# Block sums of the second feed-forward weight: from VectorE subtractions to accumulating transfers issued by GpSimd

## The chip, the cores and the metric

The kernel runs on one core of one Trainium2 chip. The metric is the device time of one execution in microseconds (us). TensorE (PE) multiplies, VectorE (DVE) and ScalarE (ACT) work element by element, GpSimd (POOL) does little in this kernel, and SyncE (SP) issues the transfers from device memory into SBUF. Each engine works through its own queue in order and waits for others through semaphores.

## What is computed

Two layers on 256 tokens of 1024 values in float32. Each layer is a feed-forward block at half weight, a token mixer (a state-space branch and a gated delta-rule branch), and a second feed-forward block; a normalisation closes the whole. Only the feed-forward blocks are touched by the change:

```python
def swiglu(x, w_in, w_out):
    gate, up = jnp.split(x @ w_in, 2, axis=-1)
    return (jax.nn.silu(gate) * up) @ w_out
...
for l in range(DEPTH):
    h = h + 0.5 * swiglu(rms_norm(h, ffn1_norm[l]), ffn1_w_in[l], ffn1_w_out[l])
    ...
    h = h + 0.5 * swiglu(rms_norm(h, ffn2_norm[l]), ffn2_w_in[l], ffn2_w_out[l])
```

`w_in` is 1024 x 5632 and `w_out` 2816 x 1024, so there are four feed-forward blocks in one execution.

## The kernel before

**Weights and forms.** Weights come as tiles of 128 x 1024 float32 (512 KB). Each product is made from two halves of a weight in the matmul's rounded type: `whi` is the tile rounded by ACT (`act(hi[:], r[:])`, line 163) and `wlo` the rest, `r - hi`, by DVE (line 170). Such a pair is called a form here. PE uses a form in three matmuls per place (`mm3`, lines 295 to 298; `mm3w`, lines 300 to 303). The forms of the whole program are listed ahead in `plan`, the tiles that have to be loaded in `stream`.

**Queues.** `take()` (line 182) hands PE the next form. It first calls `load` for the tiles that the form five places on will need and four more, and then `prep` for the forms up to five places on (`NSPL = 5`). Raw tiles lie in a ring of five (`NRAW = 5`, tile `wraw`), the halves in rings of five `whi` and five `wlo`. So a load can start when the form of the tile five loads earlier has been prepared, and a form can be prepared when PE has finished the form five places before it. SP issues all loads. A compile-time scheduler may put an instruction earlier in its engine's queue than program order if its buffer is free.

**One feed-forward block.** The string `FFN` (line 37) gives the order of the work: `f`, four forms for the first columns of `w_in`; twenty `c` (`chan_chunk`), each 48 matmuls of 256 columns on two forms; and `w_out` in between and behind.

**The seven products.** `w_out` is cut into 22 blocks of 128 rows by two halves of 512 columns. Sixteen of the row blocks are done by Winograd's form of Strassen's scheme: for a pair of 2 x 2 block products there are four weight tiles w11, w12, w22, w21 and seven products instead of eight. `A` in `FFN` makes the first four (tiles `p`, forms q0 to q3), `B` the last three (forms q4 to q6, into the accumulators `o`). There are four `A` and four `B` in a block, 16 of each in the program. A product is one form and six matmuls of 512 columns (`block_products`). Row blocks that are left over are the six `d`, each one form and twelve matmuls. The forms that have to be made of weights are, in order, w11, w12 - w11, w22 - w12, w11 - w12 + w22, then w22, w21, and w21 - (w11 - w12 + w22). These sums of weights are made in place by DVE in `prep`: `less` (line 155) overwrites one raw tile with the difference of two, once each at q0, q1, q2 and q4. w11 lies in one of four extra tiles, `wfirst` (tags y0 to y3 of `slots`, shared with the mixer), and carries the running sum from q0 to q6. w22 is loaded twice, for `A` and for `B`.

**The sums of the input** are made by `block_sums` (line 449) on DVE and split into halves. `join` (line 388) adds the four banks `p` to the residual `h`, in two steps between the `B`s.

**The tail of a block.** After the last `c` come `B d B B B` and the five last `d`, `close_blocks` (line 404): 132 matmuls of 512 columns, before the next normalisation's transposes (`hnT`). Its rows carry the tile name `o`. In the normalisation POOL computes one power (line 190), on which the next block's input waits.

Of the kernel before, what the change touches and what calls it, by code (L numbers as in the profile page):

```python
# [7 lines left out]
F32 = mybir.dt.float32  # L8
# [3 lines left out]
ALU = mybir.AluOpType  # L12
# [4 lines left out]
P = 128  # L17
# [6 lines left out]
FC = FF // 256  # L24
# [5 lines left out]
NRAW = 5  # L30
NSPL = 5
# [5 lines left out]
FFN = "f" + 8 * "c" + "A" + 4 * "c" + "A" + 4 * "c" + "A" + 2 * "c" + "A" + 2 * "c" + "BdBBBddddd"  # L37
PAIRS = [(1, 2), (3, 4), (5, 6), (7, 8)]
# [14 lines left out]
def trunk_kernel(ctx, tc, x, wst, wsm, norms, lpar, rpar, cst, out):  # L53
    nc = tc.nc
    V, A, G, PE = nc.vector, nc.scalar, nc.gpsimd, nc.tensor
# [3 lines left out]
    slots = ctx.enter_context(tc.tile_pool(name="slots", bufs=1))  # L59
# [9 lines left out]
    def tt(o, a, b, op):  # L69
        return V.tensor_tensor(out=o, in0=a, in1=b, op=op)  # L70

    def stt(o, a, s, b, op0, op1):
        return V.scalar_tensor_tensor(out=o, in0=a, scalar=s, in1=b, op0=op0, op1=op1)  # L73
# [12 lines left out]
    def trb(name):  # L86
        return trp.tile([P, 512], F32, tag="tr", name=name)
# [10 lines left out]
    plan, stream = [], []  # L98

    def plan_plain(j, n):  # L100
        for i in range(j, j + n):
            stream.append(i)
            plan.append(("d", [len(stream) - 1], len(stream)))
        return j + n

    def plan_ffn(j):


        o, j2, held = j + 4 * FC, j + 4 * FC + 22, []
        for kind in FFN:  # L110
            if kind in "fc":
                j = plan_plain(j, 4 if kind == "f" else 2)
            elif kind == "d":
                o = plan_plain(o, 1)
            else:
                if kind == "A":
                    where = [len(stream) + i for i in range(3)]
                    stream.extend(range(o, o + 3))
                    held.append((where, o + 2))
                    o += 4  # L120
                    for i, need in enumerate((2, 3, 3, 3)):
                        plan.append((f"q{i}", where, where[0] + need))
                else:
                    where, b22 = held.pop(0)
                    where += [len(stream) + 1, len(stream)]
                    stream.extend([b22, b22 + 1])
                    for i in range(4, 7):
                        plan.append((f"q{i}", where, len(stream)))
        return j2

    j0 = 0
# [1 line left out]
        j0 = plan_ffn(plan_plain(plan_ffn(j0), mix))  # L133
    assert j0 == n_dram
    n_raw = len(stream)
    first = {js[0] for kind, js, _ in plan if kind == "q0"}
    n_forms = len(plan)
    state = {"loaded": 0, "prepped": 0, "taken": 0, "last": None, "hold": False, "behind": {}, "first": 0}
    raws, halves = {}, {}

    def load(j):
        if j in first:
            r = slots.tile([P, 1024], F32, tag=f"y{state['first']}", name="wfirst")
            state["first"] = (state["first"] + 1) % 4
        else:
            r = wpool.tile([P, 1024], F32, tag="wraw", name="wraw", bufs=NRAW)
        state["last"] = nc.sync.dma_start(r[:], wst[stream[j] // 2, :, (stream[j] % 2) * 1024 :][:, 0:1024])
        raws[j] = r

    def prep(i):  # L150
        kind, js, _ = plan[i]
        hi = wpool.tile([P, 1024], F32R, tag="whi", name="whi", bufs=NSPL)
        lo = wpool.tile([P, 1024], F32R, tag="wlo", name="wlo", bufs=NSPL)

        def less(o, a, b):
            tt(raws[js[o]][:], raws[js[a]][:], raws[js[b]][:], ALU.subtract)


        r = raws[js[{"q2": 1, "q4": 4, "q5": 3}.get(kind, 0)]]
        with ExitStack() as behind:  # L160
            for ins in state["behind"].pop(i, ()):
                behind.enter_context(tc.issue_after(ins))
            act(hi[:], r[:])
            if kind == "q1":
                less(1, 2, 1)
            elif kind == "q2":
                less(0, 2, 0)
            elif kind == "q4":
                less(0, 3, 0)
            tt(lo[:], r[:], f(hi[:]), ALU.subtract)  # L170
            if kind == "q0":
                less(0, 1, 0)
        for o in {"d": (0,), "q2": (1,), "q3": (2,), "q4": (4,), "q5": (3,), "q6": (0,)}.get(kind, ()):
            raws.pop(js[o])
        halves[i] = (hi, lo)

    def ahead(key, n, fn):
        while state[key] < n:
            fn(state[key])
            state[key] += 1  # L180

    def take():
        j = state["taken"]
        state["taken"] = j + 1
        ahead("loaded", min(plan[min(j + NSPL, n_forms) - 1][2] + NRAW - 1, n_raw), load)
        ahead("prepped", min(j + 1 if state["hold"] else j + NSPL, n_forms), prep)
        return halves.pop(j)

# [199 lines left out]
    def join(pb):  # L388

        hv = [[h[:, t, n * 512 : (n + 1) * 512] for n in range(2)] for t in range(2)]  # L390
        half, u2, u4, u5 = (tmp2(n) for n in ("half", "u2", "u4", "u5"))
        act(half[:], pb[1][:], scale=0.5)
        stt(hv[0][0], pb[1][:], 0.5, hv[0][0], ALU.mult, ALU.add)
        stt(u2[:], pb[6][:], 0.5, half[:], ALU.mult, ALU.add)
        stt(u4[:], pb[5][:], 0.5, u2[:], ALU.mult, ALU.add)
        tt(hv[0][1], hv[0][1], u4[:], ALU.add)
        yield
        stt(u2[:], pb[7][:], 0.5, u2[:], ALU.mult, ALU.add)
        stt(u5[:], pb[5][:], 0.5, u2[:], ALU.mult, ALU.add)
        tt(hv[1][0], hv[1][0], u2[:], ALU.add)  # L400
        tt(hv[1][1], hv[1][1], u5[:], ALU.add)
        yield

    def close_blocks(po, stat, sums, pb, nw):
# [24 lines left out]
    def ffn(nxt):  # L429
# [10 lines left out]
        def sums(p, j):  # L440

            q, i = (p - 1) // 2, (p - 1) % 2
            if j < 3:
                b = (bsa[:], bsb3)[q % 2]
                return b[:, i, 0, j, :], b[:, i, 1, j, :]
            b = (bsc[:, 0:2], bsc[:, 2:4], bsb1, bsd[:])[q]
            return b[:, i, 0, :], b[:, i, 1, :]

        def block_sums(p, g2):

            sf = tmp2("sf")
            a11, a21, a12, a22 = (g2[:, j * P : (j + 1) * P] for j in range(4))
            s1, s2_, s3, s4 = (sf[:, j * P : (j + 1) * P] for j in range(4))
            tt(s1, a21, a22, ALU.add)
            tt(s3, a11, a21, ALU.subtract)
            tt(s2_, s1, a11, ALU.subtract)
            tt(s4, a12, s2_, ALU.subtract)
            q, i = (p - 1) // 2, (p - 1) % 2
            h3, l3 = ((bsa[:], bsb3)[q % 2][:, i, o] for o in range(2))
            h1, l1 = sums(p, 3)  # L460
            s3v = sf[:, 0 : 3 * P].rearrange("p (j t) -> p j t", j=3)
            act(h3, s3v)
            act(h1, s4)
            tt(l3, s3v, f(h3), ALU.subtract)
            tt(l1, s4, f(h1), ALU.subtract)
# [7 lines left out]
        def stat(k, t):  # L473
            return (gh[k // 8][:, k % 8, t * P : (t + 1) * P], gl[k // 8][:, k % 8, t * P : (t + 1) * P])
# [10 lines left out]
        for c in range(FC - 1):  # L485
            g2 = tmp2("g2")
            for a in range(2):
                ps = accb("fc")
                chan_chunk(ps)
                sg = s2.tile([P, S], F32, tag="ca", name="sg", bufs=2)  # L490
                act(sg[:], ps[:, 0:S], AF.Silu)
                tt(g2[:, a * S : (a + 1) * S], sg[:], ps[:, S : 2 * S], ALU.mult)
                todo = todo[1:]
                if c == 0 and a == 0:
                    bank = trb("gT")
                    for k in range(2):
                        for t in range(2):
                            PE.transpose(bank[:, k * S + t * P : k * S + (t + 1) * P], gt[t][:, k * P : (k + 1) * P], ident)
                    split(0, bank[:].rearrange("p (k t) -> p k t", k=2))
            split(2 * c + 2, g2[:].rearrange("p (k t) -> p k t", k=2))  # L500
            if c + 1 <= PAIRS[-1][-1]:
                block_sums(c + 1, g2)
            if todo[0] == "A":
                if not pb:
                    pb.update({i: trb(f"p{i}") for i in (1, 6, 5, 7)})
                four = [
                    (pb[1], lambda p: stat(2 * p, 0), PAIRS[n]),
                    (pb[5], lambda p: sums(p, 0), PAIRS[n]),
                    (pb[7], lambda p: sums(p, 2), PAIRS[n]),
                    (pb[6], lambda p: sums(p, 1), PAIRS[n]),  # L510
                ]
                block_products(four, n == 0, n == len(PAIRS) - 1)
                todo = todo[1:]
                n += 1
# [844 lines left out]
```

## Time and profile before

| | us |
|---|---|
| median of three runs | 1576.33 (1573.42 to 1577.17) |
| the profiled execution, its own time | 1574.73 |
| its span in the profile | 1573.0 |
| PE busy in the span | 1544.0 |
| DVE busy | 1254.2 |
| ACT busy | 950.7 |
| POOL busy | 53.8 |

The span is what lies between the first and the last instruction; 1.7 us lie around it. A matmul's end in the profile is modelled and the next one begins before it, so PE's busy time hides short waits. The pace of PE is read from the starts of its matmuls.

### The profile page before, as it was taken

How to read it: one execution, taken by the hardware profiler on the slowest of the kernel's cores; microseconds unless marked ns; L12 is line 12 of the kernel's file. 1: busy time of each engine (PE TensorE's matmuls, PEld its weight loads, DVE VectorE, ACT ScalarE, POOL GpSimd, SP SyncE). 2: the span in 40 equal slices, each digit the busy share in tenths (PEclk: the TensorE clock that was granted, in tenths of full speed). 3: DMA queues.
4: the chain of work that ended last, by engine and by line, in shares of the span. 5: the costliest groups of instructions: out<-in, count | busy, mean ns of one | idle time of the engine just before them, and what ended most of it. 6: DMA issues, size and time to landing. Idle time of an engine off the chain costs nothing.

```text
span 1573.0 us, 28904 instructions
## 1 busy us (share of the span) xinstructions
PE 1544.0 (98%) x11432; PEld 1393.4 (89%) x11432; DVE 1254.2 (80%) x1888; ACT 950.7 (60%) x1534; POOL 53.8 (3%) x60
## 2 busy tenths in 40 slices
PE   8999999999999999999999999999999999999997
PEld 7999779999888888999789997899998888899995
DVE  6878868967899766878777888699589987677887
ACT  5656568766666645555555566776756665455554
POOL 0000010000000000000000001010000000000000
PEclk9999999999999999999999999999999999999999
DMA  8565565553565566565765456555345556555554
GB/s 297 199 201 186 185 213 188 168 164 114 180 212 164 183 205 192 169 207 181 243 206 191 166 186 223 192 188 188 115 137 200 175 185 215 176 191 187 161 186 133
DMA packets 94221, 293.12 MB, mean 186 GB/s; under 512 B 22325, under 2 KB 23301, under 8 KB 93062
## 3 DMA queue, kind: packets, MB, share of 16 engines
q1 hardware_dynamic: 94086, 291.29, 56.5%
q8 instruction: 89, 1.46, 0.4%
q14 instruction: 46, 0.38, 0.1%
HBM read 289.33 MB, written 1.92 MB: 185 GB/s over the span
## 4 chain that ended last, share of the span: by engine, by line
PE 68%; DVE 14%; DMA 7%; issue 5%; ACT 4%; POOL 1%; SPq 0%; POOLq 0%; ACTq 0%; DVEq 0%
PE fc L301 9%; PE fc L302 9%; PE fc L303 9%; DVE wlo L70 7%; DMA wraw<-in_wst_dram 4%; PE b L298 3%; PE t L297 3%; PE t L296 2%; PE t L298 2%; PE b L297 2%; PE b L296 2%; DVE ca L73 2%; ACT whi L67 2%; PE p L297 2%; PE p L298 2%
## 5 line engine op out<-in xcount | busy, mean ns | idle before, releaser
L70 DVE TENSOR_TENSOR wlo<-wraw,whi 128x1024 fp32r<-128x1024 f32 x488 | 592.3, 1222 | 176.8 <-ACT whi L67 172.3
L67 ACT ACTIVATE whi<-wraw 128x1024 fp32r<-128x1024 f32 x488 | 511.9, 1060 | 276.9 <-PE fc L302 96.0
L301 PE MATMUL fc<-uW,whi 128*128 128x256 f32 x1280 | 359.2, 281 | 0.0
L303 PE MATMUL fc<-uW,wlo 128*128 128x256 f32 x1280 | 358.9, 280 | 0.0
L302 PE MATMUL fc<-uW,whi 128*128 128x256 f32 x1280 | 358.9, 280 | 0.0
L303 PEld LDWEIGHTS fc<-uW,wlo 128*128 128x128 f32 x1280 | 243.6, 190 | 0.0
L301 PEld LDWEIGHTS fc<-uW,whi 128*128 128x128 f32 x1280 | 241.7, 189 | 0.8
L302 PEld LDWEIGHTS fc<-uW,whi 128*128 128x128 f32 x1280 | 240.3, 188 | 0.8
L67 ACT ACTIVATE whi<-wfirst 128x1024 fp32r<-128x1024 f32 x64 | 68.0, 1062 | 65.9 <-PE fc L302 50.9
L296 PE MATMUL t<-whi,uW 128*128 128x512 f32 x256 | 102.1, 400 | 0.0
L297 PE MATMUL t<-wlo,uW 128*128 128x512 f32 x256 | 100.6, 393 | 0.4 <-DVE wlo L70 0.4
L298 PE MATMUL t<-whi,uW 128*128 128x512 f32 x256 | 100.7, 393 | 0.0
L70 DVE TENSOR_TENSOR wlo<-wfirst,whi 128x1024 fp32r<-128x1024 f32 x64 | 78.3, 1223 | 8.8 <-ACT whi L67 8.8
L296 PE MATMUL b<-whi,bh 128*128 128x512 f32 x192 | 76.3, 399 | 0.3 <-ACT bh L67 0.2
L297 PE MATMUL b<-wlo,bh 128*128 128x512 f32 x192 | 74.9, 390 | 0.0
L298 PE MATMUL b<-whi,bl 128*128 128x512 f32 x192 | 74.3, 394 | 0.6 <-DVE bl L70 0.6
L70 DVE TENSOR_TENSOR wfirst<-wraw,wfirst 128x1024 f32<-128x1024 f32 x48 | 58.7, 1222 | 19.1 <-DMA wraw<-in_wst_dram 18.7
L301 PE MATMUL xs<-uW,whi 128*128 128x256 f32 x256 | 72.7, 284 | 0.0
L297 PE MATMUL o<-wlo,gh 128*128 128x512 f32 x160 | 64.5, 403 | 7.1 <-DVE wlo L70 6.9
L303 PE MATMUL xs<-uW,wlo 128*128 128x256 f32 x256 | 71.1, 278 | 0.0
L302 PE MATMUL xs<-uW,whi 128*128 128x256 f32 x256 | 71.0, 277 | 0.0
L296 PE MATMUL o<-whi,gh 128*128 128x512 f32 x160 | 62.1, 392 | 0.3 <-ACT whi L67 0.3
(315 smaller groups left out, 3385.8 us busy)
## 6 DMA issues: line engine op xcount, KB each, us to landing
wraw<-in_wst_dram SPq DMA_DIRECT2D x504, 512.0 KB, 4.5
wfirst<-in_wst_dram SPq DMA_DIRECT2D x16, 512.0 KB, 6.1
dc<-rdram SPq DMA_DIRECT2D x8, 1024.0 KB, 8.5
nw<-in_norms_dram SPq DMA_DIRECT2D x6, 512.0 KB, 5.9
gb<-rdram SPq DMA_DIRECT2D x8, 256.0 KB, 5.5
h<-in_x_dram SPq DMA_DIRECT2D x4, 256.0 KB, 5.9
out_dram<-fo SPq DMA_DIRECT2D x4, 256.0 KB, 2.0
dq<-X SPq DMA_DIRECT2D x2, 256.0 KB, 5.4
```

The lines of the kernel that those rows point to most:

```text
L67: return A.activation(out=o, in_=i, func=func, **kw)
L70: return V.tensor_tensor(out=o, in0=a, in1=b, op=op)
L73: return V.scalar_tensor_tensor(out=o, in0=a, scalar=s, in1=b, op0=op0, op1=op1)
L296: PE.matmul(ps, lh, rh, start=start, stop=False)
L297: PE.matmul(ps, lh, rl, start=False, stop=False)
L298: return PE.matmul(ps, ll, rh, start=False, stop=stop)
L301: PE.matmul(ps, wh, mh, start=start, stop=False)
L302: PE.matmul(ps, wh, ml, start=False, stop=False)
L303: PE.matmul(ps, wl, mh, start=False, stop=stop)
```

## The change

Every sum of weights now has plus signs only, so that it can be formed by transfers that add to what lies in the destination (`accum_op=ALU.add`), issued from POOL's queue. The signs move to the sums of the input (`block_sums`) and to `join`. The forms become: q1 = w11 + w12, q0 = w11, q2 = w12 + w22, q3 = w11 + w12 + w22, q4 = w22, q5 = w21, q6 = w11 + w12 + w22 + w21.

The running sum lies in the tile `wsum` (the four y tiles again): loaded with w11 two `c` ahead of its `A` in the stream, w12 added to it by a transfer at once, w22 after q1's halves are made, w21 after q3's. A ring tile `u` is loaded with w12, and w22 is added to it. w11 is loaded a second time, for q0. So a group of seven products has five plain loads, as before, and four adding transfers; and `less` is gone. `A` now takes its forms in the order q1, q0, q2, q3. In the stream an entry is "w" (ring load), "y" (load of a sum tile) or "+" (adding transfer); the load limit counts only "w" against the ring of five.

```diff
     def plan_ffn(j):
-        o, j2, held = j + 4 * FC, j + 4 * FC + 22, []
-        for kind in FFN:
+        o, j2, begun, held = j + 4 * FC, j + 4 * FC + 22, [], []
+        spots, q = [], 0
+        for at, kind in enumerate(FFN):
+            if kind == "A":
+                spots.append(at - 2)
+        o1 = o + FFN[: FFN.index("A")].count("d")
+        for at, kind in enumerate(FFN):
+            if at in spots:
+                y = len(stream)
+                stream.extend([("y", o1 + 4 * q), ("+", o1 + 4 * q + 1, y)])
+                begun.append(y)
+                q += 1
...
+            elif kind == "A":
+                y, u = begun.pop(0), len(stream)
+                stream.extend([("w", o + 1), ("+", o + 2, u), ("w", o)])
+                plan.append(("q1", (y, o + 2), u))
+                plan.append(("q0", (u + 2,), u + 3))
+                plan.append(("q2", (u,), u + 3))
+                plan.append(("q3", (y, o + 3), u + 3))
+                held.append((y, o + 2))
+                o += 4
             else:
-                if kind == "A":
-                    where = [len(stream) + i for i in range(3)]
-                    stream.extend(range(o, o + 3))
-                    held.append((where, o + 2))
-                    o += 4
-                    for i, need in enumerate((2, 3, 3, 3)):
-                        plan.append((f"q{i}", where, where[0] + need))
-                else:
-                    where, b22 = held.pop(0)
-                    where += [len(stream) + 1, len(stream)]
-                    stream.extend([b22, b22 + 1])
-                    for i in range(4, 7):
-                        plan.append((f"q{i}", where, len(stream)))
+                y, b22 = held.pop(0)
+                stream.append(("w", b22))
+                plan.append(("q4", (len(stream) - 1,), len(stream)))
+                stream.append(("w", b22 + 1))
+                plan.append(("q5", (len(stream) - 1,), len(stream)))
+                plan.append(("q6", (y,), len(stream)))
...
+    def add_to(r, i):
+        G.dma_start(out=r[:], in_=tile_of(i), accum_op=ALU.add)
+
     def load(j):
-        if j in first:
-            r = slots.tile([P, 1024], F32, tag=f"y{state['first']}", name="wfirst")
+        kind, i = stream[j][:2]
+        if kind == "+":
+            add_to(raws[stream[j][2]], i)
+            return
+        if kind == "y":
+            r = slots.tile([P, 1024], F32, tag=f"y{state['first']}", name="wsum")
...
     def prep(i):
...
-        r = raws[js[{"q2": 1, "q4": 4, "q5": 3}.get(kind, 0)]]
+        r = raws[js[0]]
...
             act(hi[:], r[:])
-            if kind == "q1":
-                less(1, 2, 1)
-            elif kind == "q2":
-                less(0, 2, 0)
-            elif kind == "q4":
-                less(0, 3, 0)
             tt(lo[:], r[:], f(hi[:]), ALU.subtract)
-            if kind == "q0":
-                less(0, 1, 0)
...
+        if kind in ("q1", "q3"):
+            add_to(r, js[1])
+        else:
+            raws.pop(js[0])
...
-        stt(u4[:], pb[5][:], 0.5, u2[:], ALU.mult, ALU.add)
-        tt(hv[0][1], hv[0][1], u4[:], ALU.add)
+        stt(u4[:], pb[5][:], -0.5, u2[:], ALU.mult, ALU.add)
+        tt(hv[0][1], hv[0][1], u4[:], ALU.subtract)
...
-            tt(s1, a21, a22, ALU.add)
+            tt(s1, a21, a22, ALU.subtract)
             tt(s3, a11, a21, ALU.subtract)
             tt(s2_, s1, a11, ALU.subtract)
-            tt(s4, a12, s2_, ALU.subtract)
+            tt(s4, a12, s2_, ALU.add)
...
                 four = [
+                    (pb[5], lambda p: sums(p, 0), PAIRS[n]),
                     (pb[1], lambda p: stat(2 * p, 0), PAIRS[n]),
-                    (pb[5], lambda p: sums(p, 0), PAIRS[n]),
                     (pb[7], lambda p: sums(p, 2), PAIRS[n]),
                     (pb[6], lambda p: sums(p, 1), PAIRS[n]),
                 ]
```

More of the change, by code (lines that the diff above doesn't have):

```diff
@@ L101, in plan_plain @@
         for i in range(j, j + n):
-            stream.append(i)
+            stream.append(("w", i))
             plan.append(("d", [len(stream) - 1], len(stream)))
@@ L135, in trunk_kernel @@
     n_raw = len(stream)
-    first = {js[0] for kind, js, _ in plan if kind == "q0"}
+    limit = []
+    for _, _, need in plan:
+        m, room = need, NRAW
+        while m < n_raw:
+            room -= stream[m][0] == "w"
+            if not room:
+                break
+            m += 1
+        limit.append(m)
     n_forms = len(plan)
@@ L139, in trunk_kernel, with tile_of @@
     raws, halves = {}, {}
+    def tile_of(i):
+        return wst[i // 2, :, (i % 2) * 1024 :][:, 0:1024]
+    def add_to(r, i):
+        G.dma_start(out=r[:], in_=tile_of(i), accum_op=ALU.add)
     def load(j):
-        if j in first:
-            r = slots.tile([P, 1024], F32, tag=f"y{state['first']}", name="wfirst")
+        kind, i = stream[j][:2]
[4 more added lines that the diff above has]
+            r = slots.tile([P, 1024], F32, tag=f"y{state['first']}", name="wsum")
             state["first"] = (state["first"] + 1) % 4
@@ L146, in load @@
             r = wpool.tile([P, 1024], F32, tag="wraw", name="wraw", bufs=NRAW)
-        state["last"] = nc.sync.dma_start(r[:], wst[stream[j] // 2, :, (stream[j] % 2) * 1024 :][:, 0:1024])
+        state["last"] = nc.sync.dma_start(r[:], tile_of(i))
         raws[j] = r
@@ L153, in prep @@
         lo = wpool.tile([P, 1024], F32R, tag="wlo", name="wlo", bufs=NSPL)
-        def less(o, a, b):
-            tt(raws[js[o]][:], raws[js[a]][:], raws[js[b]][:], ALU.subtract)
-        r = raws[js[{"q2": 1, "q4": 4, "q5": 3}.get(kind, 0)]]
+        r = raws[js[0]]
         with ExitStack() as behind:
@@ L163, in prep @@
             act(hi[:], r[:])
-            if kind == "q1":
-                less(1, 2, 1)
-            elif kind == "q2":
-                less(0, 2, 0)
-            elif kind == "q4":
-                less(0, 3, 0)
             tt(lo[:], r[:], f(hi[:]), ALU.subtract)
-            if kind == "q0":
-                less(0, 1, 0)
-        for o in {"d": (0,), "q2": (1,), "q3": (2,), "q4": (4,), "q5": (3,), "q6": (0,)}.get(kind, ()):
-            raws.pop(js[o])
+        if kind in ("q1", "q3"):
+            add_to(r, js[1])
+        else:
+            raws.pop(js[0])
         halves[i] = (hi, lo)
@@ L184, in take @@
         state["taken"] = j + 1
-        ahead("loaded", min(plan[min(j + NSPL, n_forms) - 1][2] + NRAW - 1, n_raw), load)
+        ahead("loaded", limit[min(j + NSPL, n_forms) - 1], load)
         ahead("prepped", min(j + 1 if state["hold"] else j + NSPL, n_forms), prep)
@@ L394, in join @@
         stt(u2[:], pb[6][:], 0.5, half[:], ALU.mult, ALU.add)
-        stt(u4[:], pb[5][:], 0.5, u2[:], ALU.mult, ALU.add)
-        tt(hv[0][1], hv[0][1], u4[:], ALU.add)
+        stt(u4[:], pb[5][:], -0.5, u2[:], ALU.mult, ALU.add)
+        tt(hv[0][1], hv[0][1], u4[:], ALU.subtract)
         yield
         stt(u2[:], pb[7][:], 0.5, u2[:], ALU.mult, ALU.add)
-        stt(u5[:], pb[5][:], 0.5, u2[:], ALU.mult, ALU.add)
+        stt(u5[:], pb[5][:], -0.5, u2[:], ALU.mult, ALU.add)
         tt(hv[1][0], hv[1][0], u2[:], ALU.add)
-        tt(hv[1][1], hv[1][1], u5[:], ALU.add)
+        tt(hv[1][1], hv[1][1], u5[:], ALU.subtract)
         yield
@@ L504, in ffn @@
                 if not pb:
-                    pb.update({i: trb(f"p{i}") for i in (1, 6, 5, 7)})
+                    pb.update({i: trb(f"p{i}") for i in (5, 6, 1, 7)})
                 four = [
+                    (pb[5], lambda p: sums(p, 0), PAIRS[n]),
                     (pb[1], lambda p: stat(2 * p, 0), PAIRS[n]),
-                    (pb[5], lambda p: sums(p, 0), PAIRS[n]),
                     (pb[7], lambda p: sums(p, 2), PAIRS[n]),
```

## The prediction

> **What bounds the kernel now.** I read the page first, then the busy times by stretches, then the timelines of ACT, DVE and PE around one `A`, then the chain of waits in a tail.
>
> ```profile
> span 1573.0 us, 28904 instructions
> PE 1544.0 (98%) x11432; PEld 1393.4 (89%) x11432; DVE 1254.2 (80%) x1888; ACT 950.7 (60%) x1534; POOL 53.8 (3%) x60
> q1 hardware_dynamic: 94086, 291.29, 56.5%
> PE 68%; DVE 14%; DMA 7%; issue 5%; ACT 4%; POOL 1%; SPq 0%; POOLq 0%; ACTq 0%; DVEq 0%
> L70 DVE TENSOR_TENSOR wfirst<-wraw,wfirst 128x1024 f32<-128x1024 f32 x48 | 58.7, 1222 | 19.1 <-DMA wraw<-in_wst_dram 18.7
> L70 DVE TENSOR_TENSOR wraw<-wraw 128x1024 f32<-128x1024 f32 x16 | 19.5, 1221 | 0.1
> ```
>
> The 64 sums cost DVE 58.7 + 19.5 = 78.2 us. That would be 5% of the span if DVE set the pace. It doesn't in most places. The next rows give the stretch from the first `A`'s preparation to the first tail (PE, PEld, DVE, ACT, POOL, clock, DMA share, GB/s):
>
> ```profile
> 59.00:104.00 45.00, 45.00 (x340) 43.12 (x340) 39.32 (x56) 27.24 (x38) 0.00 (x0) 1.00 0.52 169
> 104.00:160.00 56.00, 56.00 (x432) 54.09 (x431) 46.54 (x60) 31.46 (x42) 0.00 (x0) 1.00 0.59 193
> ```
>
> PE is busy in all of it; since modelled ends hide short waits, I also compared starts, and `fc` and `p` matmuls follow each other at one pace. Here 48 of the 64 sums run (three in each `A`), and nothing is to be won by taking them away: DVE works ahead of PE, held back by the five split buffers. The pace of PE on 512 columns comes from two starts twelve matmuls apart:
>
> ```profile
> 72.00 0.39 PE L296 MATMUL p<-whi,bsa 128*128 128x512 f32 x1
> 74.73 0.39 PE L296 MATMUL p<-whi,bsa 128*128 128x512 f32 x1
> ```
>
> (74.73 - 72.00) / 12 = 0.2275 us each. With it the four tails, rows of the accumulators `o` alone (length, PE, PEld, DVE, ACT, clock, DMA share, GB/s):
>
> ```profile
> 160.20:193.00 32.80, 31.50 (x132) 24.17 (x132) 1.38 (x2) 0.00 (x0) 1.00 0.60 201
> 753.10:787.50 34.40, 31.89 (x132) 24.19 (x132) 1.38 (x2) 0.00 (x0) 1.00 0.73 253
> 937.90:970.00 32.10, 30.93 (x132) 24.26 (x132) 1.38 (x2) 0.00 (x0) 1.00 0.59 201
> 1529.00:1566.30 37.30, 34.77 (x144) 26.30 (x144) 2.08 (x4) 0.00 (x0) 1.00 0.42 138
> ```
>
> 132 matmuls need 30.0 us and 144 need 32.8, so PE loses 2.8, 4.4, 2.1 and 4.5 us: **13.8 us in the four tails**. That is all that feeding PE sooner can win here. DVE's rows in the last tail show the cause:
>
> ```profile
> 1524.93 1.23 DVE L70 TENSOR_TENSOR wfirst<-wraw,wfirst 128x1024 f32<-128x1024 f32 x1 [3.60 <-DMA wraw<-in_wst_dram]
> 1526.08 1.22 DVE L70 TENSOR_TENSOR wlo<-wraw,whi 128x1024 fp32r<-128x1024 f32 x1
> ...
> 1531.50 1.23 DVE L70 TENSOR_TENSOR wfirst<-wraw,wfirst 128x1024 f32<-128x1024 f32 x1 [0.82 <-DMA wraw<-in_wst_dram]
> ...
> 1540.79 1.23 DVE L70 TENSOR_TENSOR wfirst<-wraw,wfirst 128x1024 f32<-128x1024 f32 x1 [1.45 <-DMA wraw<-in_wst_dram]
> ```
>
> The sum for q6 needs w21. It stands in DVE's queue ahead of `wlo` tiles whose data is there, and DVE idles 3.60, 0.82 and 1.45 us until w21 lands. The late `wlo` then frees its ring tile late, and the next load starts late; the chain goes round this loop.
>
> **Part by part.** *Removed:* 64 sums of 1.22 us. 48 are hidden under PE, worth nothing. The 16 of the `B`s, 4 x 1.22 = 4.9 us of DVE in each tail, go together with the waits for w21 that stand before them. What is left for DVE in a tail's `B d B B B` is 13 `wlo` of 1.22 = 15.9 us and the eight operations of the join at this row's price,
>
> ```profile
> L73 DVE SCALAR_TENSOR_TENSOR u<-p,u 128x512 f32<-128x512 f32 x12 | 8.3, 690 | 0.1
> ```
>
> 5.5 us, together 21.4 (26.3 before). PE needs 4 x 18 + 12 = 84 matmuls = 19.1 us; the 2.3 us between them are covered by the five forms that DVE is ahead when the tail begins, 3 us at their least in the `A` rows below. If that cover were gone, a tail would keep those 2.3 us. Late next would be the ring: a lap is load, `whi` and `wlo`, by these rows
>
> ```profile
> 1519.09 5.82 DMA wraw<-in_wst_dram
> 1524.93 0.04 DVE wfirst L70
> ...
> 1535.40 5.36 DMA wraw<-in_wst_dram
> 1540.79 0.04 ACTq L67
> 1540.82 0.04 issue
> 1540.87 1.07 ACT whi L67
> 1541.94 1.42 DVE wlo L70 x2
> ```
>
> 5.8 + 1.1 + 1.2 = 8.1 us for five tiles, 1.6 us a tile, where PE takes 4.1 us for a `B`'s two tiles and 2.7 for a `d`. So the ring keeps up, and I let tails one, three and four lose all but 0.3 us: 2.5 + 1.8 + 4.2 = 8.5 us gained.
>
> *Added:* 64 adding transfers of 512 KB, 33.6 MB on 291.29. Plain loads stay five to a group. The trace before has no transfer from POOL and none that adds. The nearest rows:
>
> ```profile
> wraw<-in_wst_dram SPq DMA_DIRECT2D x504, 512.0 KB, 4.5
> wfirst<-in_wst_dram SPq DMA_DIRECT2D x16, 512.0 KB, 6.1
> dc<-rdram SPq DMA_DIRECT2D x8, 1024.0 KB, 8.5
> DMA to landing us min/median/max: 3.3/4.5/9.3
> 785.44 0.55 POOL L190 TENSOR_TENSOR zz<-zz,mhalf 128x1 f32<-128x1 f32 x1 [176.32 <-DVE zz L78]
> ```
>
> (The fourth is of the ring tiles.) From below a sum costs what the fastest load does, 3.3 us; from above twice the slowest load, 18.6, since the old value must be read too. I take 8.5 us, the row with twice the bytes, and 1.0 us for POOL's own part, about two of its smallest instructions: 9.5 us from the release to the landing. Ends kept: 4 and 20 us.
>
> The Trainium skill, in "Collectives: The Full Stack" under "The bandwidth ceiling: the fold count and why AG ≠ RS ≠ AR", says that an add made in transit reads two sources for each chunk and so runs at half a copy's rate. No row here shows it; by it the data part doubles, and by the median load an estimate of 2 x 4.5 = 9 us follows.
>
> *What waits.* The tight one is w22 added to the y tile between q1 and q3. It starts when the first form's `wlo` is done and must land before the fourth form's `whi`. Rows of the first `A`, forms one and four:
>
> ```profile
> 60.53 1.23 DVE L70 TENSOR_TENSOR wlo<-wfirst,whi 128x1024 fp32r<-128x1024 f32 x1 [0.25 <-ACT whi L67]
> ...
> 69.27 1.06 ACT L67 ACTIVATE whi<-wfirst 128x1024 fp32r<-128x1024 f32 x1 [2.05 <-PE fc L302]
> 70.73 1.06 ACT L67 ACTIVATE whi<-wraw 128x1024 fp32r<-128x1024 f32 x1 [0.40 <-PE fc L302]
> ...
> 70.37 1.23 DVE L70 TENSOR_TENSOR wlo<-wfirst,whi 128x1024 fp32r<-128x1024 f32 x1 [0.19 <-ACT whi L67]
> ```
>
> Form one ends at 61.76. The fourth waits for a split buffer until 69.27 anyway: 7.5 us in which the sum costs nothing. PE wants the fourth at 74.73, and the halves take 70.37 + 1.23 - 69.27 = 2.3 us, so it stalls only if the sum takes more than 74.73 - 2.3 - 61.8 = **10.6 us**. At 9.5 us the fourth form's halves come 2 us later and PE doesn't wait. Behind the waiting `whi` on ACT stand the next `c`'s `whi` (70.73) and the `sg` of the running `c`; they have the same 3 us. The sum into u has more: a ring tile's load is issued seven forms before q2 is prepared, and the first sum into y more again. POOL's queue holds only these transfers in a block; the power at 785.44 comes after them.
>
> *Moved:* the y loads now carry a sum each, and they go where the wfirst loads went. Before the third block that is the second tail:
>
> ```profile
> 761.29 0.33 SPq L147 DMA_DIRECT2D wfirst<-in_wst_dram  x1
> 767.86 0.33 SPq L147 DMA_DIRECT2D wfirst<-in_wst_dram  x1
> 771.87 0.33 SPq L147 DMA_DIRECT2D wfirst<-in_wst_dram  x1
> ```
>
> (the fourth at 752.37). Four sums are 2.1 MB, or 4.2 if the old value counts, in 34.4 us: 61 to 122 GB/s on 253 at a share of 0.73, so 0.91 to 1.08. I count half of this tail's gain, 2.2 us. Signs, `join` and the product order have as many instructions as before: nothing.
>
> **Sum:** 8.5 + 2.2 = 10.7 us. The profiled execution's own time, 1573.0 + 1.7 around it = 1574.7, becomes 1564.0; the median of the runs lies 1.6 higher, so 1566.
>
> **Rivals.** *The gain is given back (no change).* The tails stay short of tiles: if landings in them rise to 8 us and more by the sums, a lap takes 10.4 us, 2.1 a tile, PE's own pace in a `B`, and tails one to three keep their 9.3 us; with the fourth's 4.2 gained: 1572, or 1576 if that is lost too. For it: a share of 0.73 in the second tail. Against: tails one, three and four have no early y loads, at 0.42 to 0.60. That the change doesn't do what it says, freeing DVE where DVE isn't the bound, is the same case.
>
> *The sum into y comes late (slower).* Place: q3 in each of the 16 `A`s; each us beyond 10.6 costs 16 us, so from 11.3 us on the kernel is slower. For it: the largest landing of a plain load is already 9.3 us. At 14 us: 1576.3 + 16 x 3.4 - 10.7 = 1620; at the upper end, 20 us, about 1716. Against: most loads take half the time, and only 1.1 us of the 10.6 are missing at twice the bytes.
>
> *Transfers saturate or POOL is held up (slower).* 33.6 MB raise the mean share from 56.5% to 63%, and 70% if counted twice. By the queue's row 512 KB take 0.565 x 1573 / 291.29 x 0.524 = 1.6 us of all transfer engines. The stretch from 104 to 160 has 33 us of transfers in 56 us, and six sums come into it: at half a load's rate 19 us more, which fits; at a quarter 38 us, 15 us too many, in four blocks 62: 1576.3 + 62 - 10.7 = 1627. Against POOL being held up by DVE: its 128x2048 writes stay at one price beside DVE's work:
>
> ```profile
> L654 POOL MEMSET AT<- 128x2048 f32 x1 | 1.8, 1814 | 0.0
> L654 POOL MEMSET TT<- 128x2048 f32 x1 | 1.8, 1810 | 0.0
> ```
>
> **Chances.** Forecast 0.52 (1562 to 1571), given back 0.12, late sum 0.26, saturation 0.10. About 0.3%, 4.7 us, is what can be told from no change: faster 0.52, same 0.12, slower 0.36. The low end of the range is all 13.8 us gained and a little more, 1561. The high end reaches into the late sum to 13.5 us, 16 x 2.9 = 46 less 10.7: 1612. It leaves out half of that case, most of saturation, and little below: two in ten.
>
> **What would show it.** Right: the rows `wfirst<-wraw,wfirst` and `wraw<-wraw` gone, DVE near 1176; the tails near 30.3 us for 132 matmuls; `p` and `fc` still at one pace through every `A`; POOL's transfers landing within 10.6 us of q1's `wlo`. Wrong: PE or PEld waiting in an `A` or the `c` behind it for ACT `whi`, and ACT for a transfer into `wsum`; a DMA share near 1; tails as long as now.

## The result and the profile after

The changed kernel takes **1581.38 us** (median of five runs, 1579.78 to 1583.52); the kernel before takes 1576.85 beside it (1573.42 to 1579.58). The ratio is 1.0038, 95% interval 1.0024 to 1.0052: slower by 0.38%. The forecast was 1566 us, faster.

The page of the changed kernel first: span and busy times, the two DMA queues (packets, MB, share of 16 engines), two groups that wait for the sums, and the DMA issues (count, size, median us to landing).

```profile
span 1580.5 us, 29019 instructions
PE 1543.8 (98%) x11432; PEld 1393.2 (88%) x11432; DVE 1186.5 (75%) x1824; ACT 945.6 (60%) x1534; POOL 110.5 (7%) x124
q1 hardware_dynamic: 94086, 291.29, 55.5%
q0 software_dynamic: 9216, 33.56, 12.1%
L67 ACT ACTIVATE whi<-wsum 128x1024 fp32r<-128x1024 f32 x48 | 50.8, 1058 | 68.5 <-DMA wsum<-in_wst_dram 38.3
L165 POOL DMA_DIRECT2D wsum<-in_wst_dram x48 | 43.3, 901 | 350.8 <-DVE wlo L70 204.6
wraw<-in_wst_dram SPq DMA_DIRECT2D x504, 512.0 KB, 5.1
wsum<-in_wst_dram POOLq DMA_DIRECT2D x48, 512.0 KB, 8.4
```

The sums are gone from DVE (1254.2 to 1186.5 us busy; the prediction said 1176), as the change says. They are now 64 transfers of 8.4 us in the median, and ACT stood still for 38 us because a sum into `wsum` had not landed: a wait that the kernel before didn't have. Where it hurts is read from the `p` rows. The fourth `A` of each block, and the third of the third block (length, PE, PEld, DVE, ACT, granted clock, DMA share, GB/s; 24 matmuls need 24 x 0.2275 = 5.46 us):

```profile
141.63:150.47 8.84, 6.03 (x24) 4.24 (x24) 0.00 (x0) 0.00 (x0) 1.00 0.72 236
736.65:743.26 6.61, 5.84 (x24) 4.25 (x24) 0.00 (x0) 0.00 (x0) 1.00 0.54 190
925.95:936.47 10.52, 7.35 (x24) 4.97 (x24) 0.00 (x0) 0.00 (x0) 0.80 0.69 203
1520.85:1529.11 8.26, 6.02 (x24) 4.24 (x24) 0.00 (x0) 0.00 (x0) 1.00 0.52 182
...
908.29:915.05 6.76, 6.00 (x24) 4.24 (x24) 0.00 (x0) 0.00 (x0) 1.00 0.37 116
```

These five lose 34.2 + 6.8 - 5 x 5.46 = **13.7 us**; all other `A` blocks take 5.44 to 5.46 us. And the four tails, rows of `o`:

```profile
161.30:192.80 31.50, 30.54 (x132) 24.51 (x132) 1.38 (x2) 0.00 (x0) 1.00 0.67 221
754.50:791.60 37.10, 33.92 (x132) 26.38 (x132) 1.38 (x2) 0.00 (x0) 0.91 0.87 282
948.60:978.60 30.00, 29.95 (x132) 24.65 (x132) 1.38 (x2) 0.00 (x0) 1.00 0.65 211
1540.00:1573.60 33.60, 33.28 (x144) 26.69 (x144) 2.07 (x3) 0.00 (x0) 1.00 0.46 153
```

By the prediction's measure they lose 1.5, 7.1, 0.0 and 0.8 us, 9.4 where it was 13.8. Three tails come near the forecast, the second lost 2.7 more instead of gaining. So the change wins 4.4 us in the tails and pays 13.7 in the `A` blocks, 9.3 on balance. The two profiled spans differ by 7.5 and the medians of the runs by 4.5; the rest is not traced, and lies within what two profiles of one kernel differ by (experiment 6).

### The profile page after: what moved, and what is told of

Same layout as the page of the kernel before. It is cut to its first block, busy times and chain, and to the rows that moved or that the text cites. A ratio compares the mean times of both kernels' runs of the same rounds, so it can differ in the third digit from the quotient of the medians.

```text
span 1580.5 us, 29019 instructions
## 1 busy us (share of the span) xinstructions
PE 1543.8 (98%) x11432; PEld 1393.2 (88%) x11432; DVE 1186.5 (75%) x1824; ACT 945.6 (60%) x1534; POOL 110.5 (7%) x124
## 3 DMA queue, kind: packets, MB, share of 16 engines
q0 software_dynamic: 9216, 33.56, 12.1%
## 5 line engine op out<-in xcount | busy, mean ns | idle before, releaser
L70 DVE TENSOR_TENSOR wlo<-wraw,whi 128x1024 fp32r<-128x1024 f32 x504 | 610.7, 1220 | 212.3 <-ACT whi L67 202.8
L67 ACT ACTIVATE whi<-wraw 128x1024 fp32r<-128x1024 f32 x504 | 526.3, 1058 | 276.1 <-PE fc L321 78.2
L70 DVE TENSOR_TENSOR wlo<-wsum,whi 128x1024 fp32r<-128x1024 f32 x48 | 58.6, 1220 | 55.8 <-ACT whi L67 55.6
L67 ACT ACTIVATE whi<-wsum 128x1024 fp32r<-128x1024 f32 x48 | 50.8, 1058 | 68.5 <-DMA wsum<-in_wst_dram 38.3
L165 POOL DMA_DIRECT2D wsum<-in_wst_dram x48 | 43.3, 901 | 350.8 <-DVE wlo L70 204.6
```

Source lines behind the costliest of these rows:

```text
L67: return A.activation(out=o, in_=i, func=func, **kw)
L165: G.dma_start(out=r[:], in_=tile_of(i), accum_op=ALU.add)
```

## The experiments

Two theories stood against each other. **Late sum**: w22 reaches the y tile too late for q3, a matter of one dependency. **Traffic**: 33.6 MB of adding transfers slow every load. The tails had their own question: what did DVE's sums cost there, its time or the wait for w21? Losses in a tail are counted below as in the prediction, from the `o` rows. A row of the first three tails ends where the next transposes begin, so what PE waits for these is in it: 0.6 us in the second tail of the changed kernel, nothing in the kernel before. Some expectations count the 12 matmuls behind and the transposes between as well, about 0.7 us more for each tail.

**1. Without the late dependency.** Two ways to free q3. The first makes the sum for q1 and q3 on DVE again:

```diff
-plan.append(("q2", (u,), u + 3))
+plan.append(("q2", (u, u + 2, y), u + 3))
...
             act(hi[:], r[:])
+            if kind == "q2":
+                tt(raws[js[2]][:], raws[js[1]][:], r[:], ALU.add)
...
```

> The sum into y between q1 and q3 is made by DVE again (y = w11 + u, in q2's preparation); the other 48 adding transfers stay. Theory of the late sum: PE loses 3.4, 1.1, 6.4 and 4.1 us in the A blocks of the four FFNs of the changed kernel because this one sum lands after PE wants q3; all of it goes, so about 1581.4 - 15 = 1566 us, p matmuls back at 5.5 us for 24. Theory of traffic (33.6 MB of adding transfers slow every load): only a quarter of them is gone, so about 1577, and some of the stalls stay.

Measured: 1585.45 us, ratio 1.0077 (1.0062 to 1.0092), slower than the change itself. Neither theory gave that. DVE's timeline at the first `A` of this kernel:

```profile
61.23 0.42 DVE L70 TENSOR_TENSOR g<-sg,fc 128x256 f32<-128x256 f32 x1
67.61 1.23 DVE L70 TENSOR_TENSOR wsum<-wraw 128x1024 f32<-128x1024 f32 x1 [5.97 <-issue]
...
70.21 1.22 DVE L70 TENSOR_TENSOR wlo<-wraw,whi 128x1024 fp32r<-128x1024 f32 x1
```

The DVE sum reads u, to which w22 is still being added in transit (a transfer that POOL issued at 58.75), and it stands in DVE's queue ahead of the `wlo` of the next form. DVE idles 6 us. The edit put a new wait in the place of the old one: the `A` blocks of this kernel lose 8.8 us, where the changed kernel's lose 13.7, and its tails lose more. It doesn't decide between the theories, and why its tails lose more was not tried. The second way leaves every transfer and moves one:

```diff
-        if kind in ("q1", "q3"):
+        if kind == "q3":
+            add_to(r, js[1] - 1)
             add_to(r, js[1])
...
```

> w22 is added to y together with w21, behind q3 instead of between q1 and q3, so q3 lacks w22 in this kernel (q6 has it). All 64 adding transfers and all bytes stay; only q3 no longer waits for one. Late sum: the stalls in the A blocks go, about 1566 us. Traffic: nothing changes, about 1581 us. If both, between: the A blocks free, but longer landings of the plain loads and longer tails.

Measured: 1571.59 us, 0.9984 (0.9973 to 0.9996). Rows of `p` (fourth `A` of the third block) and of `o` in the second and third tail:

```profile
920.16:925.60 5.44, 5.44 (x24) 4.32 (x24) 0.00 (x0) 0.00 (x0) 1.00 1.03 268
...
750.00:786.70 36.70, 32.82 (x132) 25.58 (x132) 1.38 (x2) 0.00 (x0) 0.95 0.86 282
936.90:966.80 29.90, 29.89 (x132) 24.60 (x132) 1.38 (x2) 0.00 (x0) 1.00 0.72 234
```

The `A` block that took 10.5 us takes 5.44, with the DMA share at 1.03 in it. All 16 do. So the stalls there are the **late sum**, not traffic. The second tail still loses 6.7 us, 1.6 of them PE's wait for the transposes: that part is another matter.

**2. The price of adding.**

```diff
-        G.dma_start(out=r[:], in_=tile_of(i), accum_op=ALU.add)
+        G.dma_start(out=r[:], in_=tile_of(i))
```

> The changed kernel with its 64 transfers from POOL overwriting their tiles instead of adding, so the sums are left out; places, bytes fetched, waits and order stay. Late sum by the price of adding: a plain transfer lands in about 5 us (plain loads 5.1, adding ones 8.4), below the 7 to 9 us that the fourth A leaves, so the stalls in the A blocks go (15 us), the share of POOL's queue falls from 12% to about 6.5%, and the second tail loses less than 8; 1562 to 1568 us. If a transfer from POOL is as late without adding (its issue is what costs): landings of 8.4, and 1580 us.

Measured: 1564.22 us, 0.9925 (0.9914 to 0.9937), no `A` above 5.49 us. Its page:

```profile
q0 software_dynamic: 9216, 33.56, 6.7%
wsum<-in_wst_dram POOLq DMA_DIRECT2D x48, 512.0 KB, 5.1
wraw<-in_wst_dram POOLq DMA_DIRECT2D x16, 512.0 KB, 6.3
```

The same bytes in the same places land in 5.1 us instead of 8.4 and take 6.7% of the transfer engines instead of 12.1%: adding costs 3.3 us of latency and 1.8 times the engine time. With the shorter landings no `A` stalls. The second tail (not 8, but still 4.9 us lost) stays slow even so.

**3. More time ahead of the fourth `A`.**

```diff
-FFN = ... "A" + 2 * "c" + "A" + 2 * "c" + "BdBBBddddd"
+FFN = ... "A" + 4 * "c" + "A" + "BdBBBddddd"
...
-        rest = FFN[FFN.rindex("c") + 1 :]
+        rest = FFN[FFN.index("B") :]
```

> The changed kernel with its last two c put ahead of the fourth A instead of behind it, so that each A has at least four c ahead of it; sums and transfers as they are. If the fourth A stalls because two c leave only 7 to 9 us between q1's wlo and q3: A blocks at 5.5 us, about 12 to 15 us gained, 1567 to 1571 (the second tail stays at 7 to 8). If the transfers are too slow anywhere once they have piled up (the third A lost 1.3 in the third FFN): the fourth A stalls as before, 1580.

Measured: 1567.58 us, 0.9954 (0.9939 to 0.9969). The fourth `A` of the first and third block:

```profile
152.37:158.06 5.69, 5.69 (x24) 4.24 (x24) 0.00 (x0) 0.00 (x0) 1.00 0.48 148
...
928.61:934.04 5.43, 5.43 (x24) 4.32 (x24) 0.00 (x0) 0.58 (x1) 1.00 0.51 90
```

With every sum still added in transit, two `c` moved by one place take the loss away and make the change faster than the kernel before. What the fourth `A` blocks lost hung on the two `c`. The second tail was expected to stay at 7 to 8 us and loses 4.7 (749.1 to 783.8), at a DMA share of 1.03 over its whole length.

**4. The second tail.** In the changed kernel the y loads and first sums of the third block run early into it. This edit holds the loads in program order:

```diff
+            with tc.issue_after(state["last"].ins):
+                state["last"] = nc.sync.dma_start(r[:], tile_of(i))
+            raws[j] = r
+            return
```

> The loads of the y tiles are held behind the plain load that stands before them in the program, so they and their first sums can't run early into the second tail. If these are what makes the second tail lose 7.1 us (before the change 4.2): it falls to the 1 to 1.5 us of tails one and four, the power on POOL comes at its old distance, and the time is 1581.4 - 6 = 1575 to 1576 us. If the second tail is short of tiles for another reason: 7 us there as now, and 1581. If a later first sum stalls q1 in the second A: above 1582.

Measured: 1596.16 us, 1.0142 (1.0122 to 1.0161). Second tail, then the third `A` of the fourth block:

```profile
764.50:795.10 30.60, 30.28 (x132) 24.53 (x132) 1.38 (x2) 0.00 (x0) 1.00 0.68 224
...
1510.90:1523.94 13.04, 7.90 (x24) 4.89 (x24) 0.00 (x0) 0.00 (x0) 0.79 0.71 174
```

Both branches of the expectation came true: the tail falls from 7.1 us lost to 0.6, and with the y loads and first sums no longer early, later `A` blocks stall by far more (in the block shown ACT waits 4.8 us for a ring tile and 5.0 for `wsum`). A third edit tried to have both, with the order of experiment 3 and the y loads six places ahead of their `A`, in order:

```diff
-                spots.append(at - 2)
+                spots.append(at - 6)
```

> The changed kernel with the last two c ahead of the fourth A, the y loads held in program order, and their place six items ahead of their A instead of two. All 64 adding transfers stay. If the second tail lost by the y loads and first sums of the next block that ran early into it: second tail at 1.5 us or less, its granted clock at 1.00 and DMA share under 0.8; A blocks at 5.5 us if six items are enough for the first sum; 1560 to 1564 us. If the first sums come late again: the second and third A at 6 to 12 us, 1568 to 1590. If the second tail is slow for another reason: 5 us or more there as before, 1567.

Measured: 1572.24 us, 0.9990 (0.9977 to 1.0004): no difference. Its second tail, to be held against the changed kernel's:

```profile
751.90:783.70 31.80, 30.72 (x132) 24.36 (x131) 1.38 (x2) 0.00 (x0) 1.00 0.77 247
```

The tail is at 1.8 us lost, clock 1.00, share 0.77, near what was expected; but the third `A` took 6.8 to 7.8 us in three blocks, so six places are still too few there. Why tails one and three of this kernel lose 2.3 to 2.5 us was not tried.

**5. What the tails lose: time or wait.** First the kernel before with its sum moved behind w21's own form, then the same sum on POOL:

```diff
-            elif kind == "q4":
+            elif kind == "q5":
                 less(0, 3, 0)
```
```diff
-                less(0, 3, 0)
+                G.tensor_tensor(out=raws[js[0]][:], in0=raws[js[3]][:], in1=raws[js[0]][:], op=ALU.subtract)
```

> The kernel before with one edit: the sum for q6 on DVE moves from q4's preparation into q5's, ahead of q5's wlo, which needs w21 anyway. No transfer from POOL, DVE's time in a tail as before (4.9 us of sums in each). If the tails lose by the wait for w21 ahead of wlo tiles whose data is there: tails at 1 us or less, 1563 to 1567 us. If they lose by DVE's time: tails as before, 1574 to 1577.

> The same edit, and the sum for q6 is an instruction of POOL's instead of DVE's (16 of 128x1024). If DVE's time in a tail still costs something behind the wait: 1 to 3 us faster than with the sum on DVE, 1560 to 1564 us. If POOL's sum takes long or slows DVE: q6's whi late, tails at 2 us and more, 1566 to 1575.

Measured: 1575.31 us, 0.9998 (0.9988 to 1.0007), and 1572.96 us, 0.9980 (0.9967 to 0.9993). Neither gained what was hoped for; both times lie in the range that stood for the other case. For the first kernel that case was DVE's time, but its rows don't say so: the sum on DVE moved, its wait didn't. The row of these sums in the first of the two kernels, with DVE's idle time ahead of them last:

```profile
L70 DVE TENSOR_TENSOR wfirst<-wraw,wfirst 128x1024 f32<-128x1024 f32 x48 | 58.6, 1221 | 19.4 <-DMA wraw<-in_wst_dram 19.3
```

19.4 us, against 19.1 in the kernel before: w21 is the newest load at either place. The four tails lose 14.2 us. On POOL the sum is no cheap way out; three of its rows in the last tail:

```profile
1520.76 2.40 POOL L169 TENSOR_TENSOR wfirst<-wraw,wfirst 128x1024 f32<-128x1024 f32 x1 [3.07 <-DVE wlo L70]
1526.36 2.40 POOL L169 TENSOR_TENSOR wfirst<-wraw,wfirst 128x1024 f32<-128x1024 f32 x1 [3.20 <-DMA wraw<-in_wst_dram]
1537.55 7.55 POOL L169 TENSOR_TENSOR wfirst<-wraw,wfirst 128x1024 f32<-128x1024 f32 x1 [8.79 <-DMA wraw<-in_wst_dram]
```

It takes 2.4 us at best and 7.6 in a stretch where DVE is busy for 5.3 of them, and q6 waits for it; the last tail loses 5.8 us, all four 12. Then the hybrid: the changed signs, the three sums of an `A` on DVE, and w21 alone by transfer:

```diff
-            tt(raws[js[o]][:], raws[js[a]][:], raws[js[b]][:], ALU.subtract)
+            tt(raws[js[o]][:], raws[js[a]][:], raws[js[b]][:], ALU.add)
...
-            elif kind == "q4":
-                less(0, 3, 0)
...
+        if kind == "q3":
+            b21 = stream[js[2]] + 1
+            G.dma_start(out=r[:], in_=wst[b21 // 2, :, (b21 % 2) * 1024 :][:, 0:1024], accum_op=ALU.add)
...
```

> Made from the kernel before with the changed signs: the three sums of an A are DVE's again (additions), and only w21 is added to y by a transfer, behind q3; 16 adding transfers, 8.4 MB. If the wait for w21 in DVE's queue is what the tails lose: all four tails at 1 us or less (2.6, 4.2, 2.1, 4.4 before), no stall in any A, 1576.8 - 11 = 1566 us. If the tails are bound by the ring's loads and not by DVE: 1574 to 1577 us, with the tails as before.

Measured: **1561.88 us, 0.9922 (0.9908 to 0.9937)**, faster than both kernels. Its second and fourth tail:

```profile
748.60:778.80 30.20, 30.20 (x132) 24.50 (x132) 1.38 (x2) 0.00 (x0) 1.00 0.78 271
...
1520.15:1553.00 32.85, 32.85 (x144) 26.77 (x144) 2.08 (x3) 0.00 (x0) 1.00 0.44 144
```

All four tails lose 0.2 us together, and no `A` is above 5.48. In this kernel DVE's time is then put back without a wait:

```diff
+            if kind == "q4":
+                tt(lo[:], r[:], f(hi[:]), ALU.subtract)
```

> The kernel with only w21 by transfer, and in each B one DVE instruction more: q4's wlo is made twice (16 times 1.22 us, nothing waits for a load that didn't before). If what the tails of the kernel before lost was DVE's time for the sums: the tails go back to 2.5 to 4.5 us each, about 10 us slower than without it, 1570 to 1574. If it was the wait for w21: tails stay near 1 us, 1562 to 1564.

Measured: 1562.56 us, 0.9921 (0.9906 to 0.9937). 16 instructions more on DVE cost nothing that can be told in the runs; its profile's tails lose 4.1 us. Last, the kernel before with w21 as the older load, and PE's products in the same order:

```diff
-                    where += [len(stream) + 1, len(stream)]
-                    stream.extend([b22, b22 + 1])
-                    for i in range(4, 7):
+                    where += [len(stream), len(stream) + 1]
+                    stream.extend([b22 + 1, b22])
+                    for i in (5, 4, 6):
...
```

> The kernel before with w21 loaded and prepared ahead of w22 in each B (forms and products in the order q5, q4, q6); the sum for q6 stays DVE's and stays in q4's preparation, but its w21 is now the older of the two loads instead of the newest. DVE's time and the bytes as before. If the tails lose because q6 hangs on the newest load through the sum (sum on DVE or POOL alike: 16.8 and 14.6 us in four tails, against 2.8 with w21 added in transit and 6.8 with DVE's time put back without a wait): four tails at 6 to 8 us, 1564 to 1567 us. If the sum on DVE costs the same wherever its w21 comes from: tails at 14 to 17 us, 1573 to 1577.

Measured: 1565.56 us, 0.9934 (0.9920 to 0.9948). The row of the sums again, and the fourth tail:

```profile
L70 DVE TENSOR_TENSOR wfirst<-wraw,wfirst 128x1024 f32<-128x1024 f32 x48 | 58.5, 1219 | 10.6 <-DMA wraw<-in_wst_dram 10.4
...
1522.40:1557.50 35.10, 33.80 (x144) 26.52 (x144) 2.08 (x3) 0.00 (x0) 1.00 0.45 145
```

No transfer, no byte and no instruction more, only another order. DVE's wait ahead of these sums and the four tails' loss go together: 19.1 and 13.8 us before, 19.4 and 14.2 with the sum moved, 10.6 and 6.9 here, none and 0.2 in the hybrid. With DVE's time alone it is 4.1. So the **wait for w21** is the larger part of what the tails lost. By which way it costs PE is not separated: the prediction has it through DVE's queue, where the sum blocks other `wlo`, but with the sum on POOL, and DVE free of it, the tails still lost 12 us, by q6 itself coming late.

**6. The kernel before once more.**

> The kernel before, unchanged, for a second profile. In the first one the fc matmuls ran at 0.118 us each in the first seven c of FFN 1, 2 and 4 and at 0.113 in FFN 3; in the changed kernel at 0.113 in all four, some 4.5 us less. If the pace belongs to the kernel: the same four values again. If it is drawn anew in each execution: another pattern, and that part of a difference between two profiles says nothing of an edit. The four tails should lose 2.8, 4.4, 2.1 and 4.5 us again within 0.5 if waits of this kind are reproducible.

Measured: one run, 1578.36 us; the rows of `fc` in the first block, in equal windows, of the first profile, the changed kernel and this one:

```profile
28.00:64.00 36.00, 35.81 (x305) 35.63 (x304) 2.48 (x6) 2.19 (x6) 1.00 0.74 254
```
```profile
28.00:64.00 36.00, 35.81 (x315) 35.63 (x314) 2.48 (x6) 2.19 (x6) 1.00 1.02 306
```
```profile
28.00:64.00 36.00, 35.81 (x316) 35.63 (x315) 2.48 (x6) 2.19 (x6) 1.00 0.79 263
```

The pace is drawn anew: 305 matmuls in one profile of this kernel, 316 in the other, where blocks one and four were quick and two and three slow. The tails lost 2.5, 4.5, 3.7 and 3.7 us, 14.4 in sum, with 20.7 us of DVE's waits ahead of the sums; single tails moved by up to 1.6.

## Why the prediction was wrong

**What bounds the kernel, and what the tails can give: right.** The 13.8 us were there to be had, by taking the wait for w21 out of the tails; the hybrid has nearly all of them. That this wait acts through DVE's queue is not shown (experiment 5). The prediction's gain for tails one, three and four (8.5 us) came out as 1.3 + 2.1 + 3.7 = 7.1.

**The price of a sum: nearly right.** 9.5 us were taken. One case, the fourth `A` of the first block, from the timelines of DVE, POOL, ACT and PE in the changed kernel:

```profile
135.27 1.21 DVE L70 TENSOR_TENSOR wlo<-wsum,whi 128x1024 fp32r<-128x1024 f32 x1
137.01 0.88 POOL L165 DMA_DIRECT2D wsum<-in_wst_dram  x1 [5.63 <-ACT whi L67]
146.82 1.06 ACT L67 ACTIVATE whi<-wsum 128x1024 fp32r<-128x1024 f32 x1 [7.37 <-DMA wsum<-in_wst_dram]
...
145.48 0.39 PE L317 MATMUL p<-whi,bsb 128*128 128x512 f32 x1
147.93 0.50 PE L315 MATMUL p<-whi,bsb 128*128 128x512 f32 x1 [2.06 <-ACT whi L67]
```

q1's `wlo` ends at 136.48, the sum is in place by 146.82: 10.3 us, 0.8 more than was taken. From the end of q1's `wlo` to the landing the 16 sums of this kind take 6.3 to 12.1 us (median 9.4), and those of the four fourth `A` 10.1 to 12.1.

**The budget: the step that failed.** The prediction said that PE "stalls only if the sum takes more than 74.73 - 2.3 - 61.8 = 10.6 us", from the rows of the first `A`, and applied it to all 16 ("each us beyond 10.6 costs 16 us"). The first three `A` have four `c` or more ahead of them, the fourth has two. The profile before showed it, in the fourth `A` of its first block:

```profile
134.75 1.22 DVE L70 TENSOR_TENSOR wlo<-wfirst,whi 128x1024 fp32r<-128x1024 f32 x1
...
147.58 0.39 PE L296 MATMUL p<-whi,bsb 128*128 128x512 f32 x1
```

147.58 - 2.3 - 135.97 = 9.3 us. That is already less than the 9.5 us that the prediction took for the sum, so its own numbers, read at the tightest place, gave a stall, though of 0.2 us only. In the second and fourth block these 9.3 us are still there, and the sums take 10.4 and 12.1: 1.1 and 2.8 us too much, where the rows lose 1.2 and 2.8.

In the first and third block the budget itself shrank. In the first, PE wants q3 at 145.48 + 0.23 = 145.71, and 145.71 - 2.3 - 136.48 = 6.9 us are left. 10.3 - 6.9 = 3.4 us, and the block takes 8.84 - 5.46 = 3.4 more. The 2.4 us between 9.3 and 6.9 are q1's halves, which come that much later against PE's place, because ACT stood still in the third `A`:

```profile
123.17 1.06 ACT L67 ACTIVATE whi<-wraw 128x1024 fp32r<-128x1024 f32 x1 [4.17 <-DMA wraw<-in_wst_dram]
...
126.28 1.06 ACT L67 ACTIVATE whi<-wsum 128x1024 fp32r<-128x1024 f32 x1 [1.77 <-DMA wsum<-in_wst_dram]
```

The first of these waits is for the sum into u, which POOL issued at 113.61. "The sum into u has more" was the prediction's reading, and it was wrong here: this `A` had the cover to hide the wait from PE, but two `c` on, at the fourth, the time had not been made good. In the third block the same two waits are 5.17 and 2.43 us, 6.2 us are left for a sum of 10.1, and the row's granted clock of 0.80 goes with the rest of the 5.1 lost; there the third `A` stalls too, by 1.3, with a sum of 11.5 us.

Four `c` ahead of the fourth `A` (experiment 3, all but 0.2 us) or 3.3 us less landing (experiment 2) remove the stalls. So the rival of the late sum was right in mechanism and place, but its price was 5 `A` blocks at 1.2 to 5.1 us, not 16 at one excess.

**The second tail: the other step that failed.** The early y loads were seen, with a share of 0.91 to 1.08, and yet counted as half a gain. The changed kernel's stretches of 4 us there (length, PE, PEld, DVE, ACT, POOL, clock, DMA share, GB/s):

```profile
766.00:770.00 4.00, 4.00 (x19) 3.33 (x18) 4.00 (x5) 2.88 (x3) 0.00 (x0) 1.00 1.02 400
770.00:774.00 4.00, 4.00 (x19) 3.31 (x18) 3.15 (x4) 2.12 (x2) 0.86 (x1) 1.00 1.04 419
774.00:778.00 4.00, 2.86 (x12) 1.68 (x10) 2.11 (x2) 1.06 (x1) 0.86 (x1) 1.00 1.05 291
778.00:782.00 4.00, 2.49 (x6) 1.48 (x6) 1.43 (x2) 1.06 (x1) 0.00 (x0) 0.60 1.05 281
782.00:786.00 4.00, 4.00 (x12) 3.18 (x11) 0.48 (x1) 0.72 (x2) 0.00 (x0) 0.55 1.03 416
```

The transfer engines are full for 20 us (share above 1.00). Ring loads issued in or just ahead of this tail land after 4.3 to 10.2 us as far as the trace tells, in the kernel before after 3.7 to 6.3, and with the y loads in order (experiment 4, first edit) after 4.4 to 7.0. PE then runs dry, and its clock is cut. So the prediction's first rival, the gain given back by landings of 8 us and more, held in this one tail: 2.7 us lost against 2.2 forecast as gain, and gone with the loads in order. That the early y loads and their sums did it is shown; that a full set of transfer engines is the link is argued, for experiment 3's second tail, fuller still, lost 4.7 us.

The last 0.6 us of the 7.1 have a cause of their own. The prediction said that in POOL's queue the power "comes after them", the transfers, and put no price to it:

```profile
789.35 0.86 POOL L165 DMA_DIRECT2D wsum<-in_wst_dram  x1 [14.19 <-DMA wsum<-in_wst_dram]
789.91 0.88 POOL L209 TENSOR_TENSOR zz<-zz,mhalf 128x1 f32<-128x1 f32 x1
```

The power's input is ready at 788.77, but ahead of it stands a sum that waits for its y load to land. DVE's `hn` then waits 2.05 us for POOL, where it waited 0.73 in the kernel before. In experiment 1's second kernel it waits 2.98 us, and PE behind it 1.6.

**Removed work that hides: right.** The hybrid has the 48 sums of the `A` blocks on DVE again, and none of the blocks is slower for it.

## What to carry to other kernels

Read the slack of a new wait at its tightest place, not at the first: where a schedule repeats with fewer steps between (two `c` for four), the same transfer that is hidden eleven times stalls PE five times, and a wait that PE doesn't feel can still use up the slack of the next. Before a wait is paid off with traffic, look which load it waits for: making the needed load the older of two gave most of the gain without a byte more. And a prefetch that a scheduler may move early lands where the buffers are free, which can be the stretch with the fullest transfer engines.

## What the runs showed of the hardware

**An adding transfer** of 512 KB into SBUF landed in 8.4 us (median; 5.5 to 12.7) where the same transfer without adding took 5.1 (6.3 for the 16 into ring tiles), with 12.1% against 6.7% of the transfer engines for 33.56 MB. The Trainium skill ("Collectives: The Full Stack", "The bandwidth ceiling: the fold count and why AG ≠ RS ≠ AR") says of the adds of a reduce-scatter between cores that they read two sources and run at half a copy's rate; the 1.8 times measured here agrees.

**The clock after short waits.** In the second tail PE had no single wait of more than 1.3 us, but several close together; then its matmuls came at half pace:

```profile
781.12 0.63 PE L317 MATMUL o<-whi,gl 128*128 128x512 f32 x1
...
784.96 0.63 PE L317 MATMUL o<-whi,gl 128*128 128x512 f32 x1
```

Nine matmuls from start to start: 0.427 us each instead of 0.2275, with a granted clock of 0.55 in the row from 782. So 4 us of waits cost some 2 us more, an estimate from these starts. The Trainium skill ("TensorE: Matmul & The Clock Gate", "Wait — 56ns, not 53.3ns?") gives 426.7 ns for a cold matmul of 512 columns, which agrees.

**Two paces of `fc`.** The same matmuls run at 0.113 or 0.118 us in a block, and which one changes between executions of one kernel: about 1.4 us a block (36.00 / 305 against 36.00 / 316, over the 336 matmuls of seven `c`). Two single profiles can differ by some 4 us for no reason of an edit: the first profile of before was slow in three blocks, the changed kernel's in none. What draws it stays open.
